# Layer 0's MLP: the next layer's modulation in five steps a pair from the fourth pair on, and four additions of block 1's squares on POOL

## The chip, the cores and the metric

The kernel runs on one core of one Trainium2 chip. Its time is device microseconds of one execution; lower is better. The engines run side by side, each with a queue of its own that it works off in order: PE (matmuls and transposes, with its weight loads as PEld), DVE (vector work), ACT (activations and casts), POOL (a few vector operations, and the queue from which some DMAs are issued) and SP (DMAs only).

## The reference, cut to what matters

Two layers work on 1024 latent tokens and 256 context tokens of width 1024, all in fp32. Layer 0 is an mLSTM and short-convolution mixer, layer 1 is attention. Each has an MLP with 4096 hidden columns behind it, and each has six modulation vectors, which are one matrix-vector product with a 1024 x 6144 weight matrix per layer, once for the latent and once for the context conditioning:

```python
def sqrelu_mlp(h, w1, w2):
    return jnp.square(jax.nn.relu(h @ w1)) @ w2

for layer in range(DEPTH):
    mod_x = jnp.split((silu_c @ ada_w[layer] + ada_b[layer])[:, None, :], 6, axis=-1)
    mod_c = jnp.split((silu_cc @ ada_w[layer] + ada_b[layer])[None, None, :], 6, axis=-1)
    hx = rms_norm(x, norm1_g[layer]) * (1 + mod_x[1]) + mod_x[0]
    ...                                   # mixer -> y_x, y_c
    x = x + mod_x[2] * y_x
    x = x + mod_x[5] * sqrelu_mlp(rms_norm(x, norm2_g[layer]) * (1 + mod_x[4]) + mod_x[3],
                                  mlp_w1[layer], mlp_w2[layer])
    if not last:
        ...                               # the same for the context tokens with mod_c
```

The change lies in layer 0's MLP: in the norm ahead of it (the sum of squares of `rms_norm`), and in the place where layer 1's `mod_x` and `mod_c` are computed, which is beside the MLP's first matrix product `h @ w1`.

## The kernel before, in words

**Data.** Activations lie with their 1024 columns on the partitions (8 tiles of 128, `KT`), tokens along the free side: block 0 and block 1 of 512 latent tokens each, block 2 of 256 context tokens. Each fp32 product is made of three matmuls on a high and a low part of both operands: high·high (L337), high·low (L338), low·high (L339). So every operand is split first: the high part by a cast (L101, on ACT or DVE), the low part by a subtraction (L102, on DVE).

**The norm ahead of the MLP.** For blocks 2, 0, 1 in turn and for the eight column tiles m, the mixer's output is added to x on DVE (L348), ACT squares the new tile, and `square` adds that square to a running sum `acc` (L285), on DVE. After m = 7 the sum is split into `ahi` and `alo`; `stat` sums it over the partitions with two matmuls against ones and takes the inverse root on ACT (`rstd`, L297 and L298). Block 1's sums are the last; its `stat` is called as a part of the MLP, and `blocks.t2` and further operands of the MLP are made of it.

**The first product of the MLP.** `fast_fc1` takes the 32 column blocks of the hidden width in 16 pairs. For a pair it makes seven products (numbered 1 to 7, in the manner of Strassen) for the latent blocks, and smaller ones for the context. The order in a pair is 1, 2, 6, 5, 7, 3, 8, 4. The first three pairs (0 to 2) are interleaved: all their products 1, 2, 8, 9 come first, since block 1 is not normed yet, and then 6, 5, 7, 3, 4 of each. From pair 3 on the pairs follow one another. For each product, DVE and ACT prepare the weights (`w`): sums of raw weights (`ssum`, L867) where the product needs one, and the split. Up to three products are prepared ahead of PE. Raw weights come by POOL's queue (L909, three buffers). What PE puts out is combined on DVE (`c`, L867), squared on ACT (L971, L972) and stored by SP's queue (`hid`, L976). Counted from the code, one pair costs DVE 19 operations of 128x512: eight low parts, four sums of weights, three additions on output, four subtractions.

**Layer 1's modulation.** `ada_steps` is a generator: each `step` runs it on to its next `yield`. The twelve chunks of 512 columns come in the order 4, 0, 5, 6, 1, 7, 8, 2, 9, 10, 3, 11. Each chunk has five steps. The first four each load 512 KB of weights by SP's queue (L203) into `araw`, and work them into the sum `aacc0` with two DVE operations (L211 for the very first, L213 else). Chunks 0 to 3 serve the context too and have a second sum `aacc1`, so four DVE operations a load. The fifth step transposes the sums on PE (L218, four 128x128 matmuls a sum, in the PE queue between products), and DVE reduces the result (L220) and adds the bias (L221). There is one `araw` buffer here: a load can start only when the DVE operations on the one before have read it.

**Which steps stand where.** `fast_fc1` calls `extra(p, i, room)` at product i of pair p; it is called only behind the early products of pairs 0 to 2. Before, it steps the generator at i = 2, 5, 3, 4: three steps in each of pairs 0 to 2 (whose product 2 is early) and four in each later pair.

**What sets the order.** The program is not run in the order in which it is written. A scheduler with a timeline simulation of its own places all instructions of a stage on the engines' queues by when it thinks that they can start; the queues are then fixed, and each engine works its own off in order, waiting on semaphores.

Of the kernel before, what the change touches and what calls it, by code (L numbers as in the profile page):

```python
# [46 lines left out]
def trunk(ctx, tc, a, out):  # L47
    nc = tc.nc
    sp, act, dve, pool, pe = nc.sync, nc.scalar, nc.vector, nc.gpsimd, nc.tensor
# [19 lines left out]
    def psum():  # L69
        return ps_pool.tile([P, 512], F32, name="ps", tag="ps")  # L70
# [153 lines left out]
    def step(it, n=1):  # L224
        for _ in range(n):
            if next(it, "end") == "end":
                return
# [118 lines left out]
    def add_gated(xT, b, m, ps, layer, gate):  # L346
        n, w = TBS[b][1], 0 if b < 2 else 1
        dve.scalar_tensor_tensor(  # L348
            out=xT[b][:, m, :], in0=ps[:, 0:n], scalar=mod[layer][:, gate * 8 + m, w:w + 1],
            in1=xT[b][:, m, :], op0=ALU.mult, op1=ALU.add)  # L350
# [116 lines left out]
    def park(b, layer):  # L467
        t = dram.tile([P, KT, TBS[b][1]], F32, name=f"park{layer}{b}")
        for q in range(4):
            sp.dma_start(out=t[:, 2 * q:2 * q + 2, :], in_=xT[b][:, 2 * q:2 * q + 2, :])  # L470
        return t
# [346 lines left out]
    def mlstm_out(b, m, py):  # L818
        n, ms = TBS[b][1], slice(m * P, (m + 1) * P)
        for i in range(4):  # L820
            mm3(py[:, 0:n], wm[i][0][:, ms], wm[i][1][:, ms], mT[b][:, 0, i, :], mT[b][:, 1, i, :], i == 0, i == 3)
# [52 lines left out]
    def fast_fc1(layer, blocks, wp, hid_d, head, raw_tile, held, at, room, extra=lambda *_: None, ctx=None, hid_c=None, slots=()):  # L874
# [136 lines left out]
        for n, (p, i) in enumerate(seq):  # L1011
            while ready < min(n + 4, len(seq) if sums or n >= len(early) else len(early) + 2):
                load(ready - 3)
                prep(ready)
                ready += 1
            products(n, pe_ if n - 1 in at else pe)
            if n < len(early):
                if i == 1:
                    after(p, i)
                elif i == 2:  # L1020
                    late.append((p, i))
                if n in at:
                    at[n]()
                if n + 1 == len(early):
                    for x in late:
                        after(*x)
            else:
                after(p, i)
                extra(p, i, room)
# [238 lines left out]
    nbs = [Norm(np_, xT[b], b, g2, shift, tbufs=4) for b in range(3)]  # L1268
# [15 lines left out]
    for b in (2, 0, 1):  # L1284
        for m in range(KT):
            py = held.pop(0) if b == 2 else psum()
            if b < 2:
                mlstm_out(b, m, py)
            add_gated(xT, b, m, py, 0, 2)
            nbs[b].square(m)  # L1290
            if (b, m) == (0, 1):
                parked2[2] = park(2, 2)
                nbs[2].stat()
                h2 = nbs[2].apply()
                x2ctx.close()
            if (b, m) == (1, 0):
                nbs[0].stat()
                blocks.first(nbs[0])
                parked2[0] = park(0, 2)
            if b == 1:  # L1300
                part1(m)
                if m >= 4:
                    blocks.ahead(nbs[1], m - 4)
# [13 lines left out]
    def begin(p, i, room):  # L1317
        if i == 5 and fourth and p == room[1] // 3:
            t4 = fourth.pop()
            blocks.t4(t4[:, 0], t4[:, 1], lambda: wp.tile([P, 512], F32, name="c", tag="c", bufs=room[2]))  # L1320
# [2 lines left out]

    def extra(p, i, room):
        begin(p, i, room)
        if i in (2, 5, 3, 4):
            step(ada1[0])

    def end():
# [10 lines left out]
    hid_c = [dram.tile([P, GROUP, 512], F32, name=f"hidc{c}") for c in range(NPAIR // GROUP)]  # L1340
    fast_fc1(0, blocks, wp, hid_d, 3, raw_tile, 3, {1: stats, 3: lambda: blocks.t1(nbs[1]), 6: lambda: blocks.t3(nbs[1]), 11: lambda: fourth.append(end())},
             (3, 2, 6, None), extra, ctx=h2, hid_c=hid_c, slots=slots)
    step(ada1[0], 1000)
    actx.close()
# [214 lines left out]
    with opened("s", 2, PSUM) as scp, opened("st", 2, PSUM) as stp, opened("av", 2, PSUM) as avp, \  # L1559
# [103 lines left out]
        for n in range(len(pairs) + LAG):  # L1663
            i, p = divmod(n, NP)
# [45 lines left out]
    nbs = [Norm(np_, xT[b], b, g2, shift) for b in range(2)]  # L1710
# [98 lines left out]
```

## Time and profile before

| | |
|---|---|
| time, median of 3 runs | 2896.74 us (2893.89 to 2904.26) |
| the profiled execution | 2902.15 us, its span 2900.4 us, mean PE clock 0.983 |
| busy share of the span | PE 96%, PEld 80%, DVE 70%, ACT 51%, POOL 24% |
| first product of layer 0's MLP | about 642 to 1081 us of the span |

PE is busy nearly all the time, so what counts are the few microseconds in which it waits, or runs at the lower clock, in the stretch that the change touches. Product 1 of pair 4 starts at 766.0 us and the last pair ends at 1081.5 us: twelve pairs, 26.3 us each. In the windows below, each engine's busy time stands with its count of instructions in brackets; "PEclk" is the granted clock as a share of the full 2.4 GHz. In the timelines, the bracket behind a row is the time for which the engine stood idle before it, and what ended that.

### The profile page before, as it was taken

What the parts mean: (1) busy time and instruction counts of PE and PEld (TensorE: products, weight loads), DVE (VectorE), ACT (ScalarE), POOL (GpSimd) and SP (SyncE); (2) the same over time, 40 slices, a digit from 0 to 9 for tenths busy, and PEclk for the clock granted to TensorE, in tenths of its full rate; (3) what the DMA queues carried; (4) which work ended last, traced back from release to release, by engine and by line L of the source; (5) the groups of instructions that cost most, each with busy time, mean ns of one, the idle gap of its engine ahead of it and who ended that gap; (6) DMA issues with size and microseconds to landing.
All of it is one profiled execution on the core that took longest, in us unless ns stands there. A gap on an engine that the chain in (4) does not pass through costs nothing. (4 is left out here: it accounts for less than half of the span.)

```text
span 2900.4 us, 39287 instructions
## 1 busy us (share of the span) xinstructions
PE 2785.0 (96%) x14523; PEld 2306.2 (80%) x14523; DVE 2030.2 (70%) x3376; ACT 1492.3 (51%) x2556; POOL 689.9 (24%) x566
## 2 busy tenths in 40 slices
PE   7999999788999999999999999999999999999999
PEld 4788998667888888888888977777777788888887
DVE  5545581878776668778877777777755966578876
ACT  5311123555444454444556568888875655554443
POOL 2222313721000000000135545655554000000000
PEclk8999999999999999999999999999999999999999
DMA  7121651445666675324232310000016264484422
GB/s 240 51 66 45 201 157 59 123 145 148 196 197 184 189 264 193 131 80 153 95 132 66 92 48 19 19 19 19 19 52 199 71 198 152 134 300 158 149 96 108
DMA packets 194834, 360.19 MB, mean 124 GB/s; under 512 B 15206, under 2 KB 83666, under 8 KB 194642
## 3 DMA queue, kind: packets, MB, share of 16 engines
q1 hardware_dynamic: 179970, 312.59, 32.0%
q0 software_dynamic: 14672, 45.10, 6.1%
q8 instruction: 114, 1.87, 0.3%
q14 instruction: 78, 0.64, 0.1%
HBM read 260.53 MB, written 97.10 MB: 123 GB/s over the span
## 5 line engine op out<-in xcount | busy, mean ns | idle before, releaser
L338 PE MATMUL ps<-w 128*128 128x512 f32 (+1 forms) x1152 | 424.6, 369 | 0.9 <-DVE w L102 0.9
L339 PE MATMUL ps<-w 128*128 128x512 f32 (+1 forms) x1152 | 423.7, 369 | 0.0
L337 PE MATMUL ps<-w 128*128 128x512 f32 (+1 forms) x1152 | 406.1, 369 | 1.3 <-ACT w L101 1.3
L337 PE MATMUL ps<-tb,w 128*128 128x512 f32 x883 | 348.6, 396 | 8.1 <-ACT w L101 4.3
L338 PE MATMUL ps<-tb,w 128*128 128x512 f32 x888 | 350.1, 394 | 1.9 <-DVE tb L92 1.9
L339 PE MATMUL ps<-tb,w 128*128 128x512 f32 x888 | 347.0, 394 | 2.5 <-DVE w L102 2.5
L348 DVE SCALAR_TENSOR_TENSOR xT<-ps,mod,xT 128x512 f32<-128x512 f32 (+1 forms) x392 | 256.2, 694 | 91.4 <-PE ps L339 83.6
L92 DVE TENSOR_REDUCE nm<-s 128x1 f32<-128x512 f32 x372 | 217.4, 599 | 107.0 <-PE s L92 101.7
L101 ACT CAST w<-ssum 128x512 fp32r<-128x512 f32 x253 | 153.9, 619 | 252.4 <-PE ps L339 232.8
L92 POOL TENSOR_TENSOR pt<-pf,pt 128x1024 fp32r<-128x1024 f32 x96 | 230.3, 2399 | 172.5 <-ACT pt L92 172.3
L92 PE MATMUL av<-pt,vst 128*128 128x512 f32 (+1 forms) x960 | 258.2, 394 | 0.8 <-POOL pt L92 0.8
L338 PEld LDWEIGHTS ps<-w 128*128 128x128 f32 x1152 | 216.8, 188 | 40.9 <-DVE w L102 1.3
L337 PEld LDWEIGHTS ps<-w 128*128 128x128 f32 x1152 | 216.3, 188 | 41.0 <-ACT w L101 1.5
L339 PEld LDWEIGHTS ps<-w 128*128 128x128 f32 x1152 | 216.3, 188 | 38.8
L92 PEld LDWEIGHTS av<-pt,vst 128*128 128x128 f32 (+1 forms) x960 | 160.0, 171 | 56.0 <-POOL pt L92 1.2
L92 ACT ACTIVATE pf<-st 128x1024 f32<-128x1024 f32 x160 | 164.2, 1026 | 76.2 <-PE st L92 69.0
L909 POOL DMA_DIRECT2D raw<-in_mlp_w_dram x70 | 62.2, 889 | 591.8 <-DVE w L102 279.0
L337 PEld LDWEIGHTS ps<-tb,w 128*128 128x128 f32 x883 | 166.8, 189 | 45.2 <-ACT w L101 5.6
L339 PEld LDWEIGHTS ps<-tb,w 128*128 128x128 f32 x888 | 167.5, 189 | 41.6 <-DVE w L102 3.7
L338 PEld LDWEIGHTS ps<-tb,w 128*128 128x128 f32 x888 | 167.8, 189 | 37.1 <-DVE tb L92 2.8
L213 DVE SCALAR_TENSOR_TENSOR aacc<-araw,cw,aacc 128x512 f32<-128x512 f32 x196 | 145.8, 775 | 70.3 <-DMA araw<-in_ada_w_dram 69.6
L102 DVE TENSOR_TENSOR w<-ssum,w 128x512 fp32r<-128x512 f32 x253 | 171.1, 684 | 22.1 <-ACT w L101 21.5
(390 smaller groups left out, 6596.0 us busy)
## 6 DMA issues: line engine op xcount, KB each, us to landing
hid<-c SPq DMA_DIRECT2D x224, 256.0 KB
tf<-hid SPq DMA_DIRECT2D x112, 512.0 KB
araw<-in_ada_w_dram SPq DMA_DIRECT2D x72, 512.0 KB
raw<-in_mlp_w_dram POOLq DMA_DIRECT2D x70, 512.0 KB, 5.0
park<-xT SPq DMA_DIRECT2D x32, 512.0 KB
xT<-park SPq DMA_DIRECT2D x32, 512.0 KB
w2e<-in_mlp_w_dram SPq DMA_DIRECT2D x32, 512.0 KB
w2o<-in_mlp_w_dram SPq DMA_DIRECT2D x32, 512.0 KB
```

Source lines behind the costliest of these rows:

```text
L92: return lambda *args, **kw: tc.keep_in_program_order(op(*args, **kw))
L101: (hi_eng or act.copy)(out=hi, in_=src)
L102: (lo_eng or pool).tensor_tensor(out=lo, in0=src, in1=hi.bitcast(F32), op=ALU.subtract)
L213: dve.scalar_tensor_tensor(out=accs[w], in0=r[:, k, :], scalar=c, in1=accs[w], op0=ALU.mult, op1=ALU.add)
L337: pe1.matmul(ps, whi, hhi, start=start, stop=False, skip_group_check=goes_on)
L338: pe.matmul(ps, whi, hlo, start=False, stop=False, skip_group_check=goes_on)
L339: pe.matmul(ps, wlo, hhi, start=False, stop=stop, skip_group_check=goes_on)
L348: dve.scalar_tensor_tensor(out=xT[b][:, m, :], in0=ps[:, 0:n], scalar=mod[layer][:, gate * 8 + m, w:w + 1], in1=xT[b][:, m, :], op0=ALU.mu ...
L909: pool.dma_start(out=r, in_=kt_view(w1, (2 * p + e) * P, P))
```

## The change

There are two edits. In the norm of block 1, the additions of squares at m = 1, 3, 5, 7 run on POOL; those at m = 2, 4, 6 stay on DVE (m = 0 has none). And `extra` takes no steps in pairs 0 to 2, and five in each pair from pair 3 on, at i = 2, 6, 5, 3, 4.

```diff
             add_gated(xT, b, m, py, 0, 2)
-            nbs[b].square(m)
+            nbs[b].square(m, pool if b == 1 and m % 2 else dve)
...
     def extra(p, i, room):
         begin(p, i, room)
-        if i in (2, 5, 3, 4):
+        if p >= 3 and i in (2, 6, 5, 3, 4):
             step(ada1[0])
```

The instructions are the same in number, and outside of this stage they stand where they stood. On POOL, this is the place before, where the norm of block 1 goes over into the MLP (`tb` are low parts of raw weights, `raw` are loads of w1):

```order
L330 TENSOR_TENSOR t_5613<-xT2_5483,rstd_5579 128x256
L102 TENSOR_TENSOR tb_5945<-raw_5954,tb_5945 128x512 x2
L102 TENSOR_TENSOR tb_5945<-raw_5956,tb_5945 128x512 x2
L909 DMA raw_5964<-in_mlp_w1_dram 128x8x128
L909 DMA raw_5998<-in_mlp_w1_dram 128x8x128
L909 DMA raw_6066<-in_mlp_w1_dram 128x8x128
```

And this is the same place on POOL in the changed kernel:

```order
L285 TENSOR_TENSOR acc_5743<-acc_5743,sq_5816 128x512
L285 TENSOR_TENSOR acc_5743<-acc_5743,sq_5851 128x512
L285 TENSOR_TENSOR acc_5743<-acc_5743,sq_5889 128x512
L102 TENSOR_TENSOR tb_5945<-raw_5954,tb_5945 128x512 x2
L102 TENSOR_TENSOR tb_5945<-raw_5956,tb_5945 128x512 x2
L909 DMA raw_5964<-in_mlp_w1_dram 128x8x128
L285 TENSOR_TENSOR acc_5743<-acc_5743,sq_5930 128x512
L909 DMA raw_5998<-in_mlp_w1_dram 128x8x128
```

Three of the additions stand ahead of the low parts, and the fourth stands between two loads of weights.

On DVE, this is a piece of before in one of the later pairs, in a chunk with two sums (`araw_7637` is the chunk's fourth load):

```order
L213 SCALAR_TENSOR_TENSOR aacc0_7474<-araw_7637,cw_112,aacc0_7474 128x512
L213 SCALAR_TENSOR_TENSOR aacc1_7477<-araw_7637,cw_112,aacc1_7477 128x512
L213 SCALAR_TENSOR_TENSOR aacc0_7474<-araw_7637,cw_112,aacc0_7474 128x512
L213 SCALAR_TENSOR_TENSOR aacc1_7477<-araw_7637,cw_112,aacc1_7477 128x512
L867 TENSOR_TENSOR c_7610<-ps_7483,u_7587 128x512
L102 TENSOR_TENSOR w_7617<-raw_7377,w_7617 128x512
L102 TENSOR_TENSOR w_7643<-raw_7377,w_7643 128x512
L102 TENSOR_TENSOR w_7662<-ssum_7659,w_7662 128x512
L102 TENSOR_TENSOR w_7724<-ssum_7658,w_7724 128x512
L867 TENSOR_TENSOR ssum_7659<-raw_7377,ssum_7659 128x512
L867 TENSOR_TENSOR c_7632<-ps_7574,u_7567 128x512
```

This is such a chunk on DVE in the changed kernel (`araw_7077` and `araw_7125` are its third and fourth load; `w_7105`, `w_7131` and `w_7150` are weights of products 1, 2 and 6 of the pair that follows):

```order
L213 SCALAR_TENSOR_TENSOR aacc0_7027<-araw_7077,cw_112,aacc0_7027 128x512
L213 SCALAR_TENSOR_TENSOR aacc1_7030<-araw_7077,cw_112,aacc1_7030 128x512
L213 SCALAR_TENSOR_TENSOR aacc0_7027<-araw_7077,cw_112,aacc0_7027 128x512
L213 SCALAR_TENSOR_TENSOR aacc1_7030<-araw_7077,cw_112,aacc1_7030 128x512
L867 TENSOR_TENSOR c_7098<-ps_6963,u_7075 128x512
L213 SCALAR_TENSOR_TENSOR aacc0_7027<-araw_7125,cw_112,aacc0_7027 128x512
L213 SCALAR_TENSOR_TENSOR aacc1_7030<-araw_7125,cw_112,aacc1_7030 128x512
L102 TENSOR_TENSOR w_7105<-raw_6861,w_7105 128x512
L102 TENSOR_TENSOR w_7131<-raw_6861,w_7131 128x512
L213 SCALAR_TENSOR_TENSOR aacc0_7027<-araw_7125,cw_112,aacc0_7027 128x512
L102 TENSOR_TENSOR w_7150<-ssum_7147,w_7150 128x512
L213 SCALAR_TENSOR_TENSOR aacc1_7030<-araw_7125,cw_112,aacc1_7030 128x512
```

Between the third load's last reader and the fourth's first reader stands one operation; the fourth load's last readers stand among the weights of the next pair.

On PE, this is where the transposes of a chunk with two sums stand before, in the middle of pair 3 (`h2h` and `h2l` are the context's operands):

```order
L338 MATMUL ps_6779<-tb_6034,w_6740 128x512
L339 MATMUL ps_6779<-tb_6034,w_6740 128x512
L337 MATMUL ps_6792<-h2h_5582,w_6877 128x256
L338 MATMUL ps_6792<-h2l_5583,w_6877 128x256
L218 MATMUL ps_6841<-ident_75,aacc0_6638 128x128 x4
L218 MATMUL ps_6849<-ident_75,aacc1_6641 128x128 x4
L337 MATMUL ps_6880<-tb_6087,w_6776 128x512
L338 MATMUL ps_6880<-tb_6087,w_6776 128x512
```

And this is where they stand on PE in the changed kernel, at the end of a pair; `w_7105` is the weight of the next pair's product 1:

```order
L339 MATMUL ps_6963<-tb4_6330,w_7083 128x512
L339 MATMUL ps_6976<-h2h_5582,w_7083 128x256
L218 MATMUL ps_7196<-ident_75,aacc0_7027 128x128 x4
L218 MATMUL ps_7204<-ident_75,aacc1_7030 128x128 x4
L337 MATMUL ps_7215<-tb_5751,w_7105 128x512
L338 MATMUL ps_7215<-tb_5751,w_7105 128x512
L339 MATMUL ps_7215<-tb_5751,w_7105 128x512
```

The transposes now stand right ahead of product 1 of the next pair in every pair that has them.

## Rows read from the trace of the kernel before

**Rows 1.** Windows: bounds, length, busy PE, PEld, DVE, ACT, POOL, PEclk, DMA share, GB/s.

```profile
642.50:766.00 123.50, 110.18 (x542) 91.57 (x543) 107.04 (x172) 68.90 (x122) 20.41 (x19) 0.94 0.55 161
766.00:1055.10 289.10, 284.28 (x1503) 242.45 (x1502) 202.32 (x332) 130.50 (x231) 17.66 (x20) 1.00 0.61 188
```

**Rows 2.** PE's waits from 640 to 760 us: total, times, longest.

```profile
PE ps L337 <- ACT w L101: 4.3, 2, 3.5
PE ps L218 <- DVE aacc L213: 4.3, 3, 2.2
...
PE ps L339 <- DVE w L102: 2.5, 2, 2.0
...
PE ps L339 <- POOL tb L102: 1.1, 1, 1.1
```

**Rows 3.** PE's timeline in that stretch, behind its longer waits.

```profile
691.30 0.51 PE L339 MATMUL ps<-tb,w 128*128 128x512 f32 x1 [2.02 <-DVE w L102]
...
714.04 0.63 PE L218 MATMUL ps<-ident,aacc 128*128 128x128 f32 x4 [2.23 <-DVE aacc L213]
...
750.62 0.63 PE L218 MATMUL ps<-ident,aacc 128*128 128x128 f32 x4 [1.52 <-DVE aacc L213]
751.79 0.66 PE L218 MATMUL ps<-ident,aacc 128*128 128x128 f32 x4 [0.54 <-DVE aacc L213]
```

**Rows 4.** A window of one microsecond, PE alone: bounds, length, busy, PEclk, DMA.

```profile
693.00:694.00 1.00, 1.00 (x4) 0.50 1.03 358
```

**Rows 5.** POOL's and DVE's timeline where block 1's norm ends.

```profile
642.62 7.18 POOL L102 TENSOR_TENSOR tb<-raw,tb 128x512 fp32r<-128x512 f32 x4 [32.54 <-DVE acc L285]
...
645.47 1.77 DVE L102 TENSOR_TENSOR tb<-t,tb 128x512 fp32r<-128x512 f32 x1
...
650.27 0.68 DVE L102 TENSOR_TENSOR alo<-acc,ahi 128x512 fp32r<-128x512 f32 x1
...
658.14 0.69 DVE L92 TENSOR_TENSOR xT<-xT,rstd 128x512 f32<-128x512 f32 x1 [1.74 <-ACT rstd L298]
```

**Rows 6.** PE's waits from 760 to 1075 us, on the transposes.

```profile
PE ps L218 <- DVE aacc L213: 0.3, 1, 0.3
```

**Rows 7.** DVE's waits from 760 to 1075 us.

```profile
DVE aacc L213 <- DMA araw<-in_ada_w_dram: 49.3, 25, 4.9
DVE ssum L867 <- DMA raw<-in_mlp_w_dram: 23.5, 11, 4.3
DVE aacc L211 <- DMA araw<-in_ada_w_dram: 10.1, 5, 3.3
DVE c L867 <- PE ps L339: 6.3, 4, 2.6
```

**Rows 8.** DVE's timeline: runs of equal operations, for their pitch.

```profile
685.69 3.69 DVE L867 TENSOR_TENSOR c<-tb 128x512 f32<-128x512 f32 x6
...
835.60 2.74 DVE L213 SCALAR_TENSOR_TENSOR aacc<-araw,cw,aacc 128x512 f32<-128x512 f32 x4 [0.72 <-DMA araw<-in_ada_w_dram]
```

**Rows 9.** DVE's timeline: the last reads of a load, the first of the next.

```profile
859.65 1.54 DVE L213 SCALAR_TENSOR_TENSOR aacc<-araw,cw,aacc 128x512 f32<-128x512 f32 x2 [0.67 <-DMA araw<-in_ada_w_dram]
866.04 1.54 DVE L213 SCALAR_TENSOR_TENSOR aacc<-araw,cw,aacc 128x512 f32<-128x512 f32 x2 [4.85 <-DMA araw<-in_ada_w_dram]
...
953.93 0.75 DVE L213 SCALAR_TENSOR_TENSOR aacc<-araw,cw,aacc 128x512 f32<-128x512 f32 x1
...
960.38 1.54 DVE L213 SCALAR_TENSOR_TENSOR aacc<-araw,cw,aacc 128x512 f32<-128x512 f32 x2 [0.75 <-DMA araw<-in_ada_w_dram]
...
997.18 1.54 DVE L213 SCALAR_TENSOR_TENSOR aacc<-araw,cw,aacc 128x512 f32<-128x512 f32 x2 [4.59 <-DMA araw<-in_ada_w_dram]
...
1002.33 0.49 DVE L211 TENSOR_SCALAR aacc<-araw,cw 128x512 f32<-128x512 f32 x1 [0.61 <-DMA araw<-in_ada_w_dram]
```

**Rows 10.** A load of w1: POOL's issue, and DVE's first read.

```profile
871.73 0.88 POOL L909 DMA_DIRECT2D raw<-in_mlp_w_dram  x1 [12.17 <-issue]
...
877.38 0.69 DVE L867 TENSOR_TENSOR ssum<-raw 128x512 f32<-128x512 f32 x1 [3.53 <-DMA raw<-in_mlp_w_dram]
```

## The prediction

> **What bounds the kernel now.** I read the windows first, then the waits of PE, then those of DVE, then single rows of the timelines. The windows show two kinds of stretch [rows 1]. From 766 us on, pairs 4 to 14 take 289.1 us, 26.3 us each, and PE is busy for 284.3 of them at full clock: PE is the bound, and hardly 5 us can be won there. From 642.5 to 766 us, where block 1's norm ends and pairs 0 to 3 run, PE is idle for 13.3 of 123.5 us and the clock is 0.94. What PE waits for there are, above all, weights (ACT's and DVE's parts of `w`), and for 4.3 us the sums that the transposes of the modulation read [rows 2].
>
> The waits of DVE tell how near DVE is to being the bound in the later pairs. From 760 to 1075 us (315 us, twelve pairs) it waits 49.3 + 10.1 = 59.4 us for `araw`, 23.5 us for raw weights of w1, and for PE's results only 6.3 us [rows 7], half a microsecond a pair. So DVE is nearly always either working or held up by a load; it keeps pace with PE with little to spare. PE waits only 0.3 us there for a modulation sum [rows 6]: so far the transposes find their sums ready.
>
> **The change part by part.** *Norm: four additions on POOL.* DVE loses four operations at a pitch of 0.60 us (six take 3.69, the last one's end overlapping) [rows 8], 2.4 us. POOL takes about 1.8 us for one: four of its 128x512 operations took 7.18. And while they ran, a DVE operation of the same size took 1.77 us in place of 0.68 [rows 5]. So each addition on POOL takes 1.2 us longer and costs the DVE work beside it about 1 us; saving and cost cancel. What it could hurt is the end of the chain: the fourth addition stands in POOL's queue behind the four low parts, which ran from 642.6 to 649.8, and is done about 652; `alo`, done at 650.95 before, about 653.5. DVE waits for `rstd` until 658.14 [rows 5], and ACT is busy until then with a weight that came late, so 0 to 1 us of it arrives. The low parts themselves stand behind three additions, and PE waited 1.1 us for one of them [rows 2]; they may start up to 1 us later. If the DVE time saved came through whole, it would be -1.2. I take 0, bounds -1.2 and +1.
>
> *Pairs 0 to 3: fewer steps.* The order shows that chunk 4, the first one, is still put where it was: the scheduler draws its steps forward. Only chunk 0 leaves. On PE its transposes go, with their waits of 1.52 and 0.54 us [rows 3] and about 1.3 us of their own; with them some six L213 and a reduction on DVE ahead of pair 3, 4.6 us. The wait of 2.23 us at 714.04 [rows 3] is for chunk 4's sum and stays, or becomes one for the weights behind it, since DVE stands at the same load. Bounds: 0, if other waits take over, and -15, all of PE's waits for weights and sums gone (4.3 + 4.3 + 2.5, and the slow clock behind them). I take -4, nearest to the rows that surely go.
>
> *Later pairs: one whole chunk in each.* All that is left, about 43 loads, is now packed at four a pair into pairs 4 to 14; before, 36 loads stood in these 289 us, 3.3 a pair (their total wait is in rows 7). There is one `araw` buffer, so between the last read of a load and the first read of the next lies a round trip of semaphore, issue and transfer. It can be read where DVE had nothing to do in between: 866.04 - (859.65 + 1.54) = 4.85 us. Others: 997.18 + 1.54 to 1002.33 = 3.6, the shortest; 953.93 + 0.75 to 960.38 = 5.7, the longest [rows 9]. I take 4.5, between them and beside the waits of 4.59 and 4.85. In this time DVE can do only what stands between the two reads in its queue.
>
> In the changed order I count, over three pairs (one chunk with two sums, two with one), 4, 4, 1, 6, then 8, 0, 3, 5, then 5, 3, 0, 8 operations between consecutive loads. At 0.60 each against 4.5 us, the waits are 2.1 + 2.1 + 3.9 + 0.9 + 0 + 4.5 + 2.7 + 1.5 + 1.5 + 2.7 + 4.5 + 0 = 26 us. DVE's own work in three pairs: 57 operations at 0.60 = 34.2; 28 L213 at 0.67 (four take 2.74 [rows 8]) = 18.8; four L211 at 0.40 = 1.6; four reductions and their additions = 2.8; together 57.4. Sum 83.4 us, without any wait for w1. Those come to about 2 us a pair now (23.5 over eleven [rows 7]; a load takes 877.38 - 871.73 = 5.7 us from issue to first read [rows 10]), but a slower DVE leaves them more time: 0 to 6 in three pairs, I take 1. So 84.5 us against 3 x 26.3 = 78.9: +5.6 for three pairs, and DVE is the bound.
>
> It must reach PE, since PE's lead is three products of weights. The transposes stand at the end of each pair ahead of the next pair's product 1, and the last sums stand on DVE amid the weights for that next pair; PE, in order, waits there for a sum that is late, with all products behind it. Three such cycles, pairs 5 to 13: +16.8. Pair 4 loses about 2 (the chunk with two sums is drawn in there), the last pairs 1.
>
> A count by another way: 0.73 loads more a pair, each with 2.7 operations at 0.67 and a wait of 59.4 / 36 = 1.65 us, is 2.5 us a pair more for DVE; less the slack of 0.5 to 1 us a pair, +1.5 to +2 a pair and 16 to 22 for eleven.
>
> *Clock.* After a stop of 2.02 us at 691.30 [rows 3] the clock read 0.50 at 693 [rows 4], that is 1.2 GHz; after the 2.23 us at 714.04 [rows 3] it did not fall. Each such stretch loses 1 to 2 us. I take +2 for one or two of them, bounds 0 and +15 (a fall behind every second chunk).
>
> Sum: 0 - 4 + 16.8 + 3 + 2 = +18 on the profiled 2902.15 us, which lies 0.19% over the median; the same +18 on 2896.74 gives 2915 us.
>
> **The rivals.** *The loads come back fast enough.* With a round trip of 3.7 us, near the shortest [rows 9], each wait above shrinks by 0.8 us: 18 in all, the cycle is 76 us, under 78.9, and PE stays the bound. Then only the early part counts: -4 to +5, no change, 2899 us in the middle. For it: the order leaves few rows at the shortest value, but DVE today hides waits of the same kind. Against it: most plain cases read 4.6 to 4.9 [rows 9].
>
> The Trainium skill ("DMA: Bandwidth & Descriptors", section "Anatomy of one DMA — SWDGE (gpsimd) path") speaks for this rival: it gives a fixed 2.0 us and bytes at 436 GB/s for a DMA, an estimate of 3.2 us for 512 KB, by which three pairs would take about 71 us. The rows do not agree with it: 3.6 is the shortest here and 4.85 the plain case [rows 9].
>
> *Faster.* The early pairs are PE's worst stretch, 13.3 us of waits and a clock of 0.94 [rows 1]. Were chunk 0's work what makes the weights late, PE's waits for them (4.3 + 2.5 [rows 2]) would go along with those for the transposes, and the full clock would come back: -15, if the later pairs lose nothing; 2882 us. It decides if DVE's last low part ahead of pair 3 comes 2 us earlier or more. Against it: the wait at 691.30 [rows 3] lies ahead of chunk 0's work.
>
> *Slower still.* A round trip of 4.9 us gives waits of 30 to 33 us a cycle and 88 to 90 us, +30, and stops over 2 us at each end of a pair would halve the clock: 2926 to 2937 us. For it: SP's queue also holds the stores of `hid`, and the longest case is 5.7 [rows 9].
>
> *The change does not do what it says.* For chunk 4 the order shows just this: its steps are drawn forward to where they were. It is part of the sum.
>
> **How the numbers follow.** A measurement of this kernel tells some 0.5% (14 us) from no change. Chances: the forecast, DVE bound by the round trip, 0.45 (2907 to 2924); loads fast enough, 0.30; slower still, 0.18; faster, 0.07. Within 0.5% is 2882 to 2911: the fast loads and the low end of the forecast, 0.36. Faster by more: 0.06. Slower by more: 0.58. The range runs from 2894, the early gain with fast loads, to 2938, the case of 4.9 us with the clock.
>
> **What would show it.** In the changed trace from 760 us on: DVE's wait for `araw` well over 59 us (some 100); PE's wait for `aacc` up from 0.3 to 10 us or more; three pairs in 82 to 86 us, the pairs with a load right behind another the longest; product 1 of pair 4 about 4 us earlier than before; the first product's end some 18 us later. POOL's additions about 1.8 us each and `rstd` no more than 1 us late. I am wrong if DVE's round trips fall under 4 us, if PE's waits stay under 5 us after 766, or if the early pairs change by more than 8 us.

## The result, and the profile after

The changed kernel takes 2916.03 us (median of 6 runs, 2912.85 to 2921.18), the kernel before 2901.57 us (6 runs, 2893.89 to 2905.86). The ratio is 1.0056, with an interval of 1.0044 to 1.0067: slower by 13 to 19 us. The forecast was +18.

Its profiled execution took 2915.67 us, with a span of 2913.9. Where the 13.5 us between the two spans lie is read from the starts of the same matmuls in both traces. The table has the way from block 0's statistics to the first product's start, from there to product 1 of pair 4, and on to product 4 of pair 15; each kernel was profiled a second time (below), and the second trace stands in brackets:

| | before (second trace) | changed (second trace) | difference |
|---|---|---|---|
| statistics of block 0 to the first product | 23.4 (23.4) | 23.8 (23.8) | +0.4 (+0.4) |
| first product to pair 4 | 123.5 (124.6) | 117.6 (117.9) | -5.9 (-6.8) |
| pair 4 to product 4 of pair 15 | 311.2 (310.7) | 338.5 (340.7) | +27.3 (+30.0) |

The other two parts are the mixer ahead of it, which ended 5.7 us (4.5) earlier, though the order of instructions there is the same, and all behind the first product, 2.6 us (7.8) shorter. So the change costs 22 to 24 us in its own stretch (0.4 - 5.9 + 27.3, and 0.4 - 6.8 + 30.0), and 8 to 12 us less than that arrive in the span.

These are PE's waits in the changed kernel from 760 to 1100 us (total, times, longest), the counterpart of [rows 6]:

```profile
PE ps L218 <- DVE aacc L213: 18.0, 11, 3.4
PE ps L339 <- DVE w L102: 4.3, 4, 1.7
PE ps L337 <- DVE c L867: 3.2, 2, 1.6
```

The transposes, which had waited 0.3 us for their sums, now wait 18.0. These are DVE's waits from 760 to 1095 us, the counterpart of [rows 7]:

```profile
DVE aacc L213 <- DMA araw<-in_ada_w_dram: 72.0, 29, 4.9
DVE ssum L867 <- DMA raw<-in_mlp_w_dram: 22.4, 10, 3.3
DVE c L867 <- PE ps L339: 13.0, 2, 8.5
DVE aacc L211 <- DMA araw<-in_ada_w_dram: 2.2, 6, 0.6
```

For `araw` they grew from 59.4 to 74.2 us. The third row, mostly one wait of 8.5 us in the last pair (at 1089 us), is no slack in the loop. Three windows show that, each of three pairs (5 to 7, 8 to 10, 11 to 13; columns as in [rows 1]):

```profile
781.80:868.10 86.30, 78.65 (x415) 66.40 (x414) 58.81 (x98) 35.07 (x63) 5.30 (x6) 1.00 0.59 183
868.10:953.60 85.50, 79.85 (x415) 67.43 (x414) 58.76 (x99) 35.18 (x63) 5.35 (x6) 0.98 0.58 185
953.60:1040.40 86.80, 78.49 (x416) 66.34 (x414) 59.05 (x100) 35.06 (x63) 5.36 (x6) 1.00 0.58 182
```

86 us stand against 78.9 before. And these are all of DVE's waits in the first of them:

```profile
DVE aacc L213 <- DMA araw<-in_ada_w_dram: 20.0, 8, 4.9
DVE ssum L867 <- DMA raw<-in_mlp_w_dram: 6.6, 3, 2.9
DVE aacc L211 <- DMA araw<-in_ada_w_dram: 0.6, 2, 0.5
DVE c L867 <- ACT c L972: 0.2, 1, 0.2
```

58.8 busy + 20.6 + 6.6 + 0.2 = 86.2 of 86.3 us, and no wait for PE: DVE, with its two kinds of loads, is the bound. In the other two windows the same sums come to 85.5 of 85.5 and 86.7 of 86.8 us. One pair's end in the changed kernel, first on DVE, then SP's issue, then PE:

```profile
883.26 0.74 DVE L213 SCALAR_TENSOR_TENSOR aacc<-araw,cw,aacc 128x512 f32<-128x512 f32 x1
888.50 1.54 DVE L213 SCALAR_TENSOR_TENSOR aacc<-araw,cw,aacc 128x512 f32<-128x512 f32 x2 [4.50 <-DMA araw<-in_ada_w_dram]
...
893.87 0.75 DVE L213 SCALAR_TENSOR_TENSOR aacc<-araw,cw,aacc 128x512 f32<-128x512 f32 x1 [2.02 <-DMA araw<-in_ada_w_dram]
...
895.74 0.75 DVE L213 SCALAR_TENSOR_TENSOR aacc<-araw,cw,aacc 128x512 f32<-128x512 f32 x1
```

```profile
884.04 0.38 SPq L203 DMA_DIRECT2D araw<-in_ada_w_dram  x1
```

```profile
896.64 0.63 PE L218 MATMUL ps<-ident,aacc 128*128 128x128 f32 x4 [2.76 <-DVE aacc L213]
897.02 0.48 PE L337 MATMUL ps<-tb,w 128*128 128x512 f32 x1
...
898.43 0.63 PE L339 MATMUL ps<-tb,w 128*128 128x512 f32 x1
```

The read ends at 884.00, SP issues at 884.04, the data are used at 888.50. The next load takes from 890.04 to 893.87, the last sum is done at 896.49, and PE starts at 896.64, after 2.76 us of nothing. From 898 on its matmuls take 0.63 us in place of 0.39: the lower clock, which the granted clock shows as 0.50 from 899 to 901 us (window, PE alone, as in [rows 4]):

```profile
899.00:901.00 2.00, 2.00 (x7) 0.50 1.07 265
```

In pairs 0 to 3, PE's waits for sums [rows 2] are gone altogether, the 2.23 us of 714.04 [rows 3] included. These are the longest of PE's waits that are left from 636 to 754 us:

```profile
PE ps L337 <- ACT tb L101: 3.4, 1, 3.4
PE ps L337 <- ACT w L101: 3.1, 1, 3.1
PE ps L339 <- DVE w L102: 2.5, 3, 1.2
```

And this is POOL at the norm, the counterpart of [rows 5]:

```profile
618.30 1.29 POOL L285 TENSOR_TENSOR acc<-acc,sq 128x512 f32<-128x512 f32 x1 [13.93 <-ACT sq L284]
626.81 1.86 POOL L285 TENSOR_TENSOR acc<-acc,sq 128x512 f32<-128x512 f32 x1 [7.22 <-ACT sq L284]
631.28 1.61 POOL L285 TENSOR_TENSOR acc<-acc,sq 128x512 f32<-128x512 f32 x1 [2.62 <-DVE acc L285]
...
645.61 1.30 POOL L285 TENSOR_TENSOR acc<-acc,sq 128x512 f32<-128x512 f32 x1
```

The additions took 1.3, 1.9, 1.6 and 1.3 us. The first had nothing beside it on DVE. The last did not, and there it was DVE that was slowed: two operations that took 1.28 us together at 868.10 in the trace of before took 2.57:

```profile
645.50 2.57 DVE L102 TENSOR_TENSOR w<-raw,w 128x512 fp32r<-128x512 f32 x2 [0.24 <-ACT w L101]
```

### The profile page after: what moved, and what is told of

It reads as the page before. It is cut to its first block, busy times and chain, and to the rows that moved or that the text cites. A ratio compares the mean times of both kernels' runs of the same rounds, so it can differ in the third digit from the quotient of the medians.

```text
span 2913.9 us, 39317 instructions
## 1 busy us (share of the span) xinstructions
PE 2785.4 (96%) x14523; PEld 2307.1 (79%) x14523; DVE 2027.1 (70%) x3372; ACT 1490.6 (51%) x2556; POOL 704.3 (24%) x570
```

## The experiments

The theory is that the one `araw` buffer's round trips make DVE the bound as soon as four loads stand in each pair. Its chief rival is the place: transposes at each pair's end, ahead of the next pair's first product. Ratios are to runs of the kernel before on the same chip in the same session.

**Each edit alone.** The diffs are the two hunks of the change, one at a time.

> The kernel before with the norm edit alone (four of block 1's additions on POOL; the modulation's steps where they were). Theory (the loss lies in the steps; on the traces the norm edit costs 0.4 us, measured from the end of block 0's sums to the MLP's first product): within 4 us of the kernel before, PE's wait for aacc from 760 us on stays under 3 us, the later pairs stay at 26.3 us. Rival (the norm edit loads POOL and DVE and is part of the loss): 5 us or more slower. Second rival (the norm edit is what brought pair 4 forward by 11 us in the changed trace, since it also re-sorts pairs 0 to 2): 5 us or more faster.

Measured: 2897.69 us, ratio 0.9983 (0.9973 to 0.9994), some 5 us faster (2 to 8). From block 0's statistics to the first product it takes 23.8 us, +0.4 as in the changed kernel; from there to product 4 of pair 15, 432.4 against 434.7. PE's wait for sums after 760 us is 1.5 us. So the first rival falls, and the gain in time is at the edge of the theory and of the second rival. In the trace, product 1 of pair 4 starts only 2.8 us earlier, not 11, and half of that is the mixer's; from block 0's statistics to product 4 of pair 15 only 1.9 us are gained: 1.8 in pairs 0 to 3 (121.6 us against 123.5) and 0.4 behind them, less the 0.4 of the norm. The rest of the gain lies outside that stretch.

> The kernel before with the step edit alone (five steps a pair from pair 3; all additions on DVE). Theory: the whole loss is here: 12 to 20 us slower than before, PE's wait for aacc from 760 us on 15 to 21 us, three pairs of the later ones in 85 to 87 us. Rival (the loss needs both edits): under 8 us slower.

Measured: 2923.87 us, ratio 1.0082 (1.0069 to 1.0094), some 22 us slower, more than the range given and more than the whole change. Its first product takes 457.7 us to product 4 of pair 15, and the waits after 760 us are those of the changed kernel:

```profile
PE ps L218 <- DVE aacc L213: 15.6, 10, 3.3
PE ps L339 <- DVE w L102: 4.0, 3, 2.3
```

The loss lies in the steps, all of it; that the time differs from the changed kernel's by 8 us comes mostly from pairs 0 to 3 (121.5 us against 117.6) and the mixer (3 us). In pairs 0 to 3 PE waits for no sum here either, but it waits longer for ACT's part of weights, 7.6 us where it was 4.3 before [rows 2] and 3.1 in the changed kernel:

```profile
PE ps L337 <- ACT w L101: 7.6, 2, 5.1
```

**Place against rate.** The steps go one place on, four loads a pair as in the changed kernel:

```diff
-        if p >= 3 and i in (2, 6, 5, 3, 4):
+        if p >= 3 and i in (2, 6, 5, 3, 4) and (p, i) != (3, 2):
```

> The changed kernel with the steps one place later: pair 3 begins at product 6, so that a chunk's four loads come at 6, 5, 3, 4 and its transposes only at product 2 of the next pair; the rate stays at four loads a pair. Theory (round trips of the one araw buffer make DVE the bound): DVE's wait for araw stays over 65 us, three pairs stay at 83 to 87 us, PE's wait for aacc turns into waits for weights or for c, and the time is within 6 us of the changed kernel, over 2908. Rival (the place of the transposes at the pair's end is what costs): PE's waits go, three pairs take 79 us, and the time falls by 15 us or more, to 2901 or less.

Measured: 2909.32 us, ratio 1.0025 (1.0014 to 1.0036). PE's waits from 760 us on, and three pairs (7 to 9):

```profile
PE ps L218 <- DVE aacc L213: 18.0, 13, 3.0
PE ps L337 <- DVE c L867: 1.1, 2, 0.8
```

```profile
838.20:924.60 86.40, 80.06 (x414) 67.16 (x413) 59.24 (x98) 35.75 (x64) 5.71 (x7) 0.98 0.60 183
```

The transposes now stand behind product 2 or 6, and wait just as long. The place is not the cause. DVE's wait for `araw` is 65.6 us from 760 to 1095 us, just over the 65 expected. The theory was wrong on one point (the wait did not turn into one for weights), and the time is 6.7 us under the changed kernel's, a little more than allowed: pairs 4 and 5 take 25.6 and 26.1 us in place of 27.0 and 28.8, since the packed chunks begin later.

**The loads taken away.** `ada_steps` loads 512 KB once, and all the other steps read the same buffer (the diff is cut to its core):

```diff
+                if raw_tile and (ch, q) != (chunks[0], 0):
+                    fresh = False
+                else:
+                    fresh = True
                     r = raw_tile() if raw_tile else p.tile(...)
+                if fresh:
                     sp.dma_start(out=r, in_=...)
```

> The changed kernel with a single load of modulation weights: the first 512 KB are loaded, all 48 steps with loads read that same buffer, and the other 47 loads are left out (so layer 1's modulation is another). DVE's and PE's work and the place of the transposes stay. Theory (the round trips of the one buffer): without them DVE needs 57 us of 79 for three pairs, PE is the bound, three pairs take 76 to 79 us, PE's wait for aacc stays under 3 us, and the time is 22 to 32 us under the changed kernel, 2886 to 2894. Rival (DVE's own work, or the transposes at the pair's end): three pairs stay over 82 us, and the time within 10 us of the changed kernel.

Measured: 2890.23 us, ratio 0.9960 (0.9949 to 0.9972), 26 us under the changed kernel. Pairs 5 to 7 and 8 to 10:

```profile
788.80:865.80 77.00, 77.00 (x413) 66.21 (x412) 58.41 (x98) 36.48 (x64) 5.30 (x6) 1.00 0.40 123
865.80:943.00 77.20, 77.20 (x416) 66.37 (x414) 58.45 (x98) 36.56 (x65) 5.31 (x6) 1.00 0.39 121
```

DVE is as busy as with the loads (58.4 us), the transposes stand at the same pairs' ends (in three chunks one of the four is drawn ahead of product 4), and PE never waits. This settles it: not the amount of DVE's work and not the place, but the loads. Two things go along with them: their traffic (the DMA share falls from 0.59 to 0.40), and the order on DVE, where the scheduler places the reads of `araw` anew. What the waits cost in the changed kernel's own order stands in its sum above. The same edit in the kernel before:

> The kernel before with a single load of modulation weights: all steps with loads read that first buffer, the other 47 loads are left out (so layer 1's modulation is another). Theory (only the loads' round trips make the two places of the steps differ): within 4 us of the changed kernel with one load, 2886 to 2895, where with loads the two stand 14 us apart. Rival (the place of the steps has a price of its own, by DVE's work in pairs 0 to 2 or by the transposes): 6 us or more from it, to either side.

Measured: 2886.29 us, ratio 0.9953 (0.9940 to 0.9967). With loads the changed kernel is 14 us slower than before; without them the two stand 4 us apart (2 by the ratios, 2.3 in the traces' first product), within the theory's limit.

**Two half buffers.** The same room and the same bytes, but two buffers of 256 KB, each loaded by a DMA of its own (the diff is cut to its core):

```diff
-                r = raw_tile() if raw_tile else p.tile(...)
-                sp.dma_start(out=r, in_=...[q * 256:(q + 1) * 256, ...])
+                r = [half(), half()]
+                for k in range(2):
+                    sp.dma_start(out=r[k], in_=...[q * 256 + k * P:q * 256 + (k + 1) * P, ...])
```

> The changed kernel with two araw buffers of half the size (256 KB loads, two per step; the same bytes and the same room), so that one half can be loaded while the other is read. Theory (round trips): DVE's wait for araw falls from 74 us to under 45, PE's wait for aacc from 18 to under 5, three pairs take 79 to 80 us, and the time falls by 18 to 28 us, to about 2892, under the kernel before. Rival (place of the transposes): within 5 us of the changed kernel. Second rival (twice as many DMAs on SP's queue make each slower): DVE's wait stays over 65 us and the time within 5 us of the changed kernel.

Measured: 2897.15 us, ratio 0.9988 (0.9979 to 0.9996), 19 us under the changed kernel. PE's wait for sums is 0.9 us from 756 us on; it waits 8.9 for DVE's `c`. DVE's wait for `araw` is still 51.6 us (under 45 expected), and three pairs take 80.7 and 82.0 (79 to 80 expected):

```profile
779.10:859.80 80.70, 77.98 (x415) 66.45 (x413) 57.87 (x97) 34.77 (x61) 4.45 (x6) 1.00 0.62 193
859.80:941.80 82.00, 77.90 (x416) 66.46 (x414) 58.61 (x99) 35.65 (x63) 5.28 (x6) 1.00 0.61 193
```

DVE's timeline there shows why (the line number is shifted by six):

```profile
873.67 0.74 DVE L219 SCALAR_TENSOR_TENSOR aacc<-araw,cw,aacc 128x512 f32<-128x512 f32 x1
...
875.54 0.74 DVE L219 SCALAR_TENSOR_TENSOR aacc<-araw,cw,aacc 128x512 f32<-128x512 f32 x1
877.37 0.75 DVE L219 SCALAR_TENSOR_TENSOR aacc<-araw,cw,aacc 128x512 f32<-128x512 f32 x1 [1.08 <-DMA araw<-in_ada_w_dram]
879.66 0.75 DVE L219 SCALAR_TENSOR_TENSOR aacc<-araw,cw,aacc 128x512 f32<-128x512 f32 x1 [1.55 <-DMA araw<-in_ada_w_dram]
```

From the end of one half's read to the next read of that half: 877.37 - 874.41 = 3.0 us, 879.66 - 876.28 = 3.4. A whole load took 3.8 and 4.5 in the rows above, so half the bytes save about 1 us. The 19 us gained are at the low end of the 18 to 28 expected; DVE's wait and the pairs miss their ranges: the mechanism is confirmed, its size was put too high.

**Combinations.** The half buffers with the norm edit and the steps of before; then the half buffers in the changed kernel with its sixty steps spread over pairs 3 to 15:

```diff
+        if p >= 3 and i in ((2, 6, 5, 3, 4) if (p - 2) * 60 // 13 - (p - 3) * 60 // 13 == 5 else (2, 5, 3, 4)):
```

> The kernel before with the norm edit and the two half buffers, the steps where they were before (3.3 loads a pair). Theory: the later pairs lose their last waits (4.6 us) at most and DVE gets slack, so 5 to 9 us faster than before, 2893 to 2897, and 0 to 5 us faster than the norm edit alone. Rival (twice as many DMAs cost SP and DVE as much as the halves win): no faster than the norm edit alone, 2898 or over.

Measured: 2895.51 us, ratio 0.9977 (0.9962 to 0.9993), the fastest complete kernel here, as expected against before. The trace agrees (429.7 us to product 4 of pair 15), but from the norm edit alone at 0.9983 it can't be told apart.

> The changed kernel with the two half buffers, and its sixty steps spread evenly over pairs 3 to 15 (five in eight of the pairs, four in the other five), about 3.7 loads a pair. Theory (rate): DVE's loads fit between, three pairs take 78.5 to 80 us, and the freed pairs 0 to 2 stay: 4 to 8 us faster than the half buffers at five a pair, 2889 to 2893, the fastest so far. Rival (the rate no longer matters with half buffers): within 3 us of five a pair, 2894 to 2900.

Measured: 2903.09 us, ratio 1.0004 (0.9994 to 1.0015): a miss for both. In its trace the first product is in fact shorter than at five a pair, 432.0 against 436.9 us, as the theory has it, though three pairs take 82.2, 77.8 and 80.0 us and not 78.5 to 80. But its mixer ended 6.4 us later (601.3 against 594.8 us), which outweighs that in these two executions.

**The kernels a second time.** That mixer, ahead of every edit, differed in all the traces, so both kernels were profiled again.

> The kernel before, unchanged, profiled a second time. In the five traces so far the mixer of layer 0, ahead of everything that the change touches, ended at 602.8 us in the kernel before (start of the norm's inverse root) and at 594.8 to 601.4 in the others, whose order there is the same. Theory (this differs from one execution to the next): it ends at another time here, by 2 us or more from 602.8. Rival (it belongs to the kernel): it ends within 1 us of 602.8.

> The changed kernel, profiled a second time. The step from the first product of the MLP to the last pair's last product took 456.1 us in its first trace, against 434.7 and 435.3 in two traces of before. Theory (the loss in this stretch belongs to the kernel): 453 to 460 us. On the mixer's end ahead of it (597.1 us in its first trace, 602.8 and 602.6 in the two of before, in the same order of instructions): if it belongs to the kernel, 597 again within 1 us; if it differs by execution, another time.

Measured: the mixer of before ended at 602.6 us, after 602.8; that of the changed kernel at 598.2, after 597.1. The others lie between 594.8 and 601.9. Two executions of one kernel agree within 1.1 us at this place, different kernels differ by up to 8. That speaks for a property of the kernel, against what was put forward as the theory for the kernel before. But it is not shown: on the way there, the changed kernel's two executions stand up to 4 us apart, at about 545 us, and the runs of the kernel before spread over 13 us (2891.9 to 2905.3). What makes the difference is open, since the order of instructions there is the same. The first product took 458.5 us in the changed kernel's second trace, inside the 453 to 460 expected.

## Why the prediction was right, point by point

*Norm.* Forecast 0, bounds -1.2 and +1; measured +0.4 up to the first product and +0.5 up to block 1's `rstd`. Up to there it was right. The edit alone made the whole kernel 2 to 8 us faster, though, outside these bounds: the prediction had no term for what it does behind the norm, in pairs 0 to 3, where its trace shows 1.8 us.

*Pairs 0 to 3.* Forecast -4; measured -5.9 and -6.8. What was wrong is the step that the wait of 2.23 us at 714.04 "stays, or becomes one for the weights behind it": it went. The order puts chunk 4's loads where they were, but its transposes at the end of pair 3, at 754 us, by which time the sum is ready. So all 4.3 us of PE's waits for sums left, and the transposes of chunk 0's two sums with them. But that is not the whole account: with the steps alone these waits left too, and this part was only 2.0 us shorter, because there waits for weights grew, as the prediction had feared. The other 3.9 us came with the norm edit, by one trace of each kernel; how is not shown.

*Later pairs.* Forecast +16.8 + 3 + 2 = +21.8; measured +27.3 and +30.0. The mechanism is as forecast: DVE bound by the loads, no slack against PE, the stop seen at the transposes (18.0 us for "10 us or more"). The sum for three pairs, 84.5 us, came out at 85.5 to 86.8, but of other terms: waits for `araw` of 20 us and not 26, for w1 of 6.6 and not 1, work of 58.8 and not 57.4. I took 4.5 us for every round trip. Of the 35 loads that DVE stood waiting for from 756 us on, 24 were read 3.6 to 3.9 us after the last read of the one before, five after 4.5 to 4.9, and six after 5.9 to 7.0; the mean is 4.4. In the six long ones DVE first did other work or waited for w1, so little of them shows as a wait for `araw`; this is one, its last read, its issue and its first read:

```profile
900.85 0.75 DVE L213 SCALAR_TENSOR_TENSOR aacc<-araw,cw,aacc 128x512 f32<-128x512 f32 x1
```

```profile
901.63 0.47 SPq L203 DMA_DIRECT2D araw<-in_ada_w_dram  x1
```

```profile
904.94 0.69 DVE L867 TENSOR_TENSOR ssum<-raw 128x512 f32<-128x512 f32 x1 [2.13 <-DMA raw<-in_mlp_w_dram]
...
907.62 0.75 DVE L213 SCALAR_TENSOR_TENSOR aacc<-araw,cw,aacc 128x512 f32<-128x512 f32 x1 [0.79 <-DMA araw<-in_ada_w_dram]
```

So the "some 100 us" of DVE's wait were 74. And w1 does not get ahead of a late DVE: ten of POOL's twenty issues of its loads from 760 to 1090 us were released by DVE's `w` (the others by ACT). Two errors of 5.5 us in three pairs cancelled each other. By place, pairs 5 to 13 cost +21.1 us (16.8 and the clock's 2 were forecast), pair 4 +1.4 (2), pair 14 +3.7 and pair 15 +1.1 (1 for both). The step that was furthest off is the last one: pair 14 holds a whole chunk like the nine before it, and was not counted as one of them.

*Clock.* Forecast +2. In the first trace the clock fell after two of the longest stops, and each cost 1.3 to 1.6 us: right. In the second it fell after three.

*The rivals.* "The loads come back fast enough" failed by its own number: at 3.7 us the cycle should have been 76 us, and most round trips were near that; the waits for w1 and the few long round trips filled the room. So the prediction's own sign of being wrong, round trips under 4 us, was there in 24 of 35, and the mechanism held all the same. The Trainium skill ("DMA: Bandwidth & Descriptors", section "Anatomy of one DMA — SWDGE (gpsimd) path") would have 3.2 us for 512 KB and, as an estimate from its formula, 2.6 us for 256 KB. The traces disagree with both: mostly 3.6 to 4.9 and, in two cases read, 3.0 and 3.4 us, from the last read to the next, here on SP's queue. The section is on the other queue's path.

*The total.* +18 forecast, +14.5 measured between the medians: closer than its terms. The stretch itself lost 22 to 24 us; the mixer and what follows the first product were shorter, which no step of the prediction knew of. That the total came so near is in this part luck.

## What to carry to other kernels

With one buffer, a load costs its engine the whole round trip less what stands between the last read and the next first read in that engine's queue: count those operations in the order before moving steps closer together. An engine that is 70% busy is the bound when the rest of its time is waits for loads, and the test is whether busy time and load waits add up to the loop. Taking the loads away, and leaving all work in, tells in one run whether place, work or loads cost, if the order that the scheduler then makes is looked at too.

## What the runs showed of the hardware that was not expected

The same stop did not always halve the clock. In the changed kernel's first trace PE stopped for 2.76 us before 896.64 and the clock fell to 1.2 GHz; it stopped for 2.77 us before 981.75 and the next matmuls ran at full speed. In the second trace both of these places, stops of 2.81 and 2.74 us, were followed by the lower clock. And an unchanged stretch, the mixer, ended up to 8 us apart in traces of kernels that differ only behind it, for a reason that stays open, so that differences in time under 0.3% between such kernels say little without the traces.
